# Modulation products moved from TensorE to VectorE, complex products by three real ones, and a new hand-written order in a one-layer S5, attention and MoE block

## The chip, the cores and the metric

The kernel runs on one core of a Trainium2 chip. The metric is the device time of one execution in microseconds; all numbers below are of that core. The engines are named as the profile names them: PE (TensorE matmul) with PEld (its weight load), DVE (VectorE), ACT (ScalarE), POOL (GpSimd) and SP (SyncE, which here only issues DMAs).

## The reference, cut to what matters

```python
def reference(x, c, ctx, c_ctx, w_mod, b_mod, w_in, s5_..., w_exp_gate, w_exp_up, w_exp_down, ...):
    sh1, sc1, g1, sh2, sc2, g2 = split(silu(c) @ w_mod + b_mod, 6)           # 6 x 1024 values
    sh1c, sc1c, ... = split(silu(c_ctx) @ w_mod + b_mod, 6)                  # only the first two are used
    h, hc = _modulate(x, sh1, sc1), _modulate(ctx, sh1c, sc1c)               # 256 x 1024 each
    u, q, k, v, gate_logits = split(h @ w_in); uc, _, kc, vc, _ = split(hc @ w_in)
    y_ssm = u * s5_d
    for d, reverse in enumerate((False, True)):                              # complex, 32 groups x 64 states
        ab, bb = _s5_discretise(a, log_dt, b)                                # powers of ab, products with b and c
        hc_ = _s5_scan(uc, ab, bb, reverse)                                  # context first ...
        hl_ = _s5_scan(u, ab, bb, reverse, init=hc_[edge])                   # ... its last state starts the latent scan
        y_ssm += real(c * hl_)
    o = attention(rope(rms(q)), [rope(rms(k)), rms(kc)], [v, vc])            # 8 heads, 2 kv heads, 512 keys
    mix = (sig(gate_s) * glu(gelu(y_ssm)) + sig(gate_a) * (o @ w_attn_o)) @ w_out
    x = _layer_norm(alpha * x + g1 * mix) * ln1_g + ln1_b
    x = _layer_norm(alpha * x + g2 * moe(_modulate(x, sh2, sc2))) * ln2_g + ln2_b   # 32 experts, top 2
    return x
```

So `sh2, sc2, g1, g2` (four of the six thousands of columns of `w_mod`) are wanted for `c` alone. Every weight is float32.

## The kernel before, in words

The 256 latent tokens are kept in two tiles of 128. There are two parts.

**The front** is the token sub-layer. It is written as 44 Python generators, each a chain of steps on some engines (`loads`, `mod1`, `mod2`, `u_flow` inside `dense`, `s5_powers`, `w1_flow`, `scan`, ...). `Flow.run` takes them by the list `Flow.ORDER`, 900 numbers long: each number says which generator takes its next step. Nothing is scheduled at run time: the list fixes the order of the instructions on every engine and of the DMAs on the queue of SP, and each engine works through its instructions in that order and waits at the head where data or a buffer is missing. Buffers are slots of a few tags: `p8` (5 of 8 KB a partition), `p4` (`N4` = 15 of 4 KB), `p2` (`N2` = 6 of 2 KB), `pe`, `t2`, and the weight slots `raw` (3 of 8 KB), `w`, `l4`, `g4` (4 each of 4 KB).

- `dense` is the main stream of matmuls: 264 steps, in this order: `u_flow` (steps 0 to 20), the k/v columns (to 52), q (to 84), the gate logits (to 156), the GLU (to 196), the attention output (to 232), the output projection (to 264). Its weights come by `loads` (SP) into `raw`, and `splits` makes a high and a low part of each (ACT copies, DVE subtracts), so that a product takes three matmuls.
- `mod_load`, `mod_loads`, `modmm`, `mod_cols`, `mod1`, `mod2`: the modulation. `w_mod` is loaded in blocks of 256 columns, and TensorE multiplies each by a 32-column tile `scp` that holds silu(c) and silu(c_ctx); ACT copies the result (`mr`), TensorE transposes it, and DVE reduces it into `modT`. `mod1` does the first 2048 columns (4 calls of `mod_cols`), `mod2` the other 4096 (8 calls, 16.8 MB, loaded into `g4`, in the trace `g<-in_w_mod_dram`).
- `s5_powers` makes powers of the diagonal (`pw`, `pin`, `pout`) and `bb`; `w2_flow` and `w1_flow` multiply them with the S5 matrices c and b, 8 blocks each, six DVE instructions of 512 elements a block (four products, two sums); `w1T_flow` transposes `w1` on TensorE, `state_in` multiplies with `U` (the S5 input, turned through HBM by `u_turn` on the queue of POOL), `scan` runs on DVE (a tree, then 31 steps in series), `states` copies, `k_flow` and `outputs` make the S5 output, which passes through HBM (`yscr`), gelu and into the GLU of `dense`.
- `scores`, `softmax`, `weigh`, `values` are the attention, worked in beside the rest; `residual`, `norm`, `stats`, `router`, `choose`, `gate1`, `diag2` the end of the front.
- `prefetch8`, `prefetch4`, `refill` load expert weights (`ew`) into slots that the front no longer needs.

**The MoE** is a plain loop over 16 pairs of experts (`for p in range(NP)`): gate and up products (`gu`), the down product (`y`), dispatch and combine. Each pair takes 12.6 MB of float32 weights; 201 MB in all go through a ring of all the slots (`first`), loaded by SP in the order of use as slots come free.

Of the kernel before, what the change touches and what calls it, by code (L numbers as in the profile page):

```python
# [8 lines left out]
FT = mybir.dt.float32  # L9
# [3 lines left out]
AF = mybir.ActivationFunctionType  # L13
# [19 lines left out]
N8, N4, N2, NPE = 5, 15, 6, 5  # L33
# [52 lines left out]
class Flow:  # L86
# [213 lines left out]
def build(ctx, tc, I, out):  # L300
# [88 lines left out]
    wm, loaded = [], []  # L389
# [15 lines left out]
    def loads():  # L405
# [1540 lines left out]
```

## Time and profile before

| | before |
|---|---|
| median of 3 runs | 819.25 us (819.23 to 820.12) |
| the profiled execution, device time | 820.36 us |
| its span, first to last instruction | 818.6 us (1.76 us lie around it) |
| mean granted clock of TensorE | 0.978 |
| PE / PEld / DVE / ACT / POOL busy | 94% / 53% / 45% / 36% / 4% |
| bytes moved by DMA | 269.73 MB, mean 330 GB/s |

A busy PE is not PE at its peak, since matmuls are pipelined and the recorded ends overlap. DVE's 45% is a mean of two unlike parts: it is near full in the first 100 us and little used in the MoE. The strip below the totals on the page (40 slices) shows that, and that DMA has gaps in the front and none after it.

### The profile page before, as it was taken

To read this page: it belongs to the slowest core of one execution; us is meant where nothing else is said; L and a number is where in the kernel's file an instruction comes from. 1 tells how busy PE (TensorE), PEld (TensorE's weight loads), DVE (VectorE), ACT (ScalarE), POOL (GpSimd) and SP (SyncE) were. 2 spreads that over 40 slices of the span, in tenths; PEclk is the share of its full clock that TensorE was granted. 3 is DMA by queue.
4 is the path that set the end of the run, shared out by engine and by line. 5 is a ranking of instruction groups with operands and counts; after the bars stand their busy time and mean duration, and the time that the engine had idled before them with its cause. 6 is when DMAs were issued, how large, how long until landed. Compare 5 with 4: busy or idle time off the path is not lost. (4 is left out here: it accounts for less than half of the span.)

```text
span 818.6 us, 11438 instructions
## 1 busy us (share of the span) xinstructions
PE 765.9 (94%) x4371; PEld 437.5 (53%) x4371; DVE 371.6 (45%) x857; ACT 295.3 (36%) x574; POOL 30.8 (4%) x48
## 2 busy tenths in 40 slices
PE   3999989989999999899999999999999999999994
PEld 1787777646667787644443444344344534444431
DVE  7999969877544767813211221122122122202115
ACT  5553586756988544522210221022022102202200
POOL 0004202000000000200000000000000000000000
PEclk9899999999999999899999999999999999999997
DMA  9977275593658686989999999999999999999992
GB/s 359 349 307 279 52 238 147 216 323 106 192 144 309 249 292 219 348 329 399 414 412 413 412 414 413 412 413 412 411 413 412 411 414 412 413 413 409 412 408 84
DMA packets 71138, 269.73 MB, mean 330 GB/s; under 512 B 12195, under 2 KB 17699, under 8 KB 59173
## 3 DMA queue, kind: packets, MB, share of 16 engines
q1 hardware_dynamic: 65268, 265.29, 83.7%
q0 software_dynamic: 1152, 2.59, 1.1%
q10 hardware_dynamic: 4656, 1.05, 0.6%
q8 instruction: 37, 0.61, 0.3%
q14 instruction: 25, 0.20, 0.1%
HBM read 265.79 MB, written 3.11 MB: 329 GB/s over the span
## 5 line engine op out<-in xcount | busy, mean ns | idle before, releaser
L238 PE MATMUL gu<-ew,x 128*64 128x512 f32 x1024 | 233.0, 602 | 4.4 <-PEq L1719 2.5
L238 PEld LDWEIGHTS gu<-ew,x 128*64 128x64 f32 x1024 | 75.3, 138 | 149.7 <-issue 134.5
L238 PE MATMUL y<-ew,hT 128*64 128x512 f32 x512 | 113.5, 595 | 0.8 <-DVE hT L238 0.8
L238 DVE TENSOR_TENSOR hh<-hh,gu 128x512 f32<-128x512 f32 x16 | 11.0, 688 | 212.1 <-PE gu L238 212.1
L238 ACT ACTIVATE x<-y,modT 128x128 f32<-128x128 f32 x120 | 45.1, 455 | 139.4 <-PE y L238 139.4
L238 DVE TENSOR_TENSOR wl<-raw,wh 128x1024 fp32r<-128x1024 f32 x52 | 63.4, 1223 | 28.7 <-ACT wh L238 28.5
L238 PEld LDWEIGHTS y<-ew,hT 128*64 128x64 f32 x512 | 36.3, 137 | 66.7 <-issue 63.6
L238 ACT ACTIVATE wh<-raw 128x1024 fp32r<-128x1024 f32 x52 | 54.9, 1059 | 25.2 <-PE acc L238 24.9
L238 PEld LDWEIGHTS y<-d,xh 128*128 128x128 f32 x480 | 55.9, 192 | 12.2 <-issue 10.5
L238 PE MATMUL acc<-wh,hh 128*128 128x512 f32 x128 | 57.3, 448 | 3.1 <-DVE q L238 2.0
L238 PE MATMUL y<-d,xh 128*128 128x128 f32 x480 | 60.0, 278 | 0.0
L238 ACT ACTIVATE yh<-x 128x512 fp32r<-128x512 f32 x32 | 20.1, 629 | 105.0 <-DVE x L238 105.0
L238 DVE SCALAR_TENSOR_TENSOR x<-y,wsl,g 128x512 f32<-128x512 f32 x32 | 24.0, 751 | 66.7 <-PE y L238 66.7
L238 ACT ACTIVATE hh<-gu 128x512 f32<-128x512 f32 x16 | 9.6, 597 | 123.4 <-PE gu L238 123.4
L238 PE MATMUL acc<-wh,hl 128*128 128x512 f32 x128 | 51.4, 401 | 0.0
L238 PE MATMUL acc<-wl,hh 128*128 128x512 f32 x128 | 51.3, 401 | 0.0
L238 DVE TENSOR_TENSOR yl<-x,yh 128x512 fp32r<-128x512 f32 x32 | 22.2, 692 | 24.1 <-ACT yh L238 24.1
L238 PEld LDWEIGHTS acc<-wh,hh 128*128 128x128 f32 x128 | 24.4, 190 | 11.8 <-issue 4.3
L238 PEld LDWEIGHTS acc<-wh,hl 128*128 128x128 f32 x128 | 24.5, 191 | 5.9
L238 PEld LDWEIGHTS acc<-wl,hh 128*128 128x128 f32 x128 | 24.5, 192 | 5.7 <-issue 1.2
L238 PE MATMUL acc<-yh,cw 128*128 128x512 f32 x64 | 27.0, 422 | 0.4 <-ACT yh L238 0.4
L238 PE MATMUL acc<-yl,cw 128*128 128x512 f32 x64 | 25.3, 395 | 0.2 <-DVE yl L238 0.2
(263 smaller groups left out, 1052.8 us busy)
## 6 DMA issues: line engine op xcount, KB each, us to landing
ew<-in_w_exp_gate_dram SPq DMA_DIRECT2D x92, 512.0 KB, 11.7
ew<-in_w_exp_up_dram SPq DMA_DIRECT2D x88, 512.0 KB, 11.4
ew<-in_w_exp_down_dram SPq DMA_DIRECT2D x84, 512.0 KB, 11.4
ew<-in_w_exp_down_dram SPq DMA_DIRECT2D x21, 1024.0 KB, 12.6
ew<-in_w_exp_up_dram SPq DMA_DIRECT2D x20, 1024.0 KB, 12.6
ew<-in_w_exp_gate_dram SPq DMA_DIRECT2D x18, 1024.0 KB, 12.5
g<-in_w_mod_dram SPq DMA_DIRECT2D x32, 512.0 KB, 6.7
raw<-in_w_in_dram SPq DMA_DIRECT2D x14, 1024.0 KB, 5.7
```

Of the source, the lines that this page charges most:

```text
L238: return f(*args, **kw)
```

## The change

- `mod2` no longer uses TensorE. `w_mod`'s last 4096 columns are stored transposed (`w_modT`), so that a tile of 128 partitions holds 128 columns, one a partition, with all 1024 weights of each along it. silu(c) is broadcast to all partitions (`cb`), and one DVE `tensor_tensor_reduce` of 128x1024 for each of 32 tiles multiplies and sums. The tiles are 512 KB each, in `p4`; the bytes are the same 16.8 MB.
- `w2_flow` and `w1_flow`: a complex product by three real products. A block now takes three DVE instructions (one of 512 elements, two of 1024). The operands for it (`pq`, `pin`, `pout`, `pone`, `sums`) are new: two additions on POOL, twelve copies of half the partitions on ACT in the place of four on DVE, two sums on DVE.
- The scratch for DMAs issued from POOL (`dynamic_dma_scratch_size`) goes from its default of 16 KB a partition to 2 KB; `N4` goes from 15 to 18, `N2` from 6 to 7.
- `prefetch4` runs over `(N4 - 4) // 2` pairs of tiles, so 7 pairs in the place of 5.
- The attention output product may start on its first half (`o_n[0] >= 2*(k//4)+2`).
- `ORDER` is another list, 895 numbers long.

```diff
-N8, N4, N2, NPE = 5, 15, 6, 5
+N8, N4, N2, NPE = 5, 18, 7, 5
...
-    ORDER = [1, 5, 1, 3, 4, 3, ...]
+    ORDER = [3, 1, 1, 3, 3, 4, ...]
...
     def mod_loads():
-        for o in ((3, 4), (2, 5)):
-            for jp in range(4):
-                yield ask("Z", None, lambda: m_l[0] == 4, lambda: U, g4=4)
-                wm.append([[wload(w_mod, z * D + 256 * jp, 256, k0, 4, "g4") for k0 in (0, 4)] for z in o])
+        for z in (1, 2, 0, 3):
+            for j in range(KT):
+                yield ask("Z", None, lambda: m_l[0] == 4, lambda: g_n[0] >= 15, p4=1)
+                r = new("p4", [P, D], name="wr")
+                SY.dma_start(r, I["w_modT"][z * KT + j])
+                wm2.append(r)
...
     def mod2():
-        for half in (1, 2):
-            for jp in range(4):
-                yield ask("T", None, lambda: mod_n[0] >= 4)
-                yield from mod_cols(half, jp)
+        yield ask("Y", None, lambda: m_l[0] == 4, lambda: g_n[0] >= 14, p4=1)
+        cb = new("p4", [P, D], name="cb")
+        bcast(cb, I["crow"], D)
+        yield ask("S", [cb], table=AF.Silu)
+        S.activation(cb, cb, AF.Silu)
+        for half, w in ((1, 0), (1, 1), (2, 0), (2, 1)):
+            sm = small.tile([P, KT], FT, name=f"msum{half}{w}", bufs=1)
+            for j in range(KT):
+                yield ask("V", lambda: [wm2[0], cb], lambda: wm2)
+                r = wm2.pop(0)
+                V.tensor_tensor_reduce(out=r, in0=r, in1=cb, scale=1.0, scalar=0.0, op0=OP.mult, op1=OP.add, accum_out=sm[:, j:j + 1])
+                free(r)
+            stt(modT[:, half, w, :, 0], sm, float(w if half < 2 else 0), bmodT[:, half, w], OP.add, OP.add)
+            md.add((half, w))
+        free(cb)
...
+        PL.tensor_tensor(out=pq[:, 0], in0=pw[:, 0], in1=pw[:, 1], op=OP.add)
+        PL.tensor_tensor(out=pq[:, 1], in0=pw[:, 1], in1=pw[:, 0], op=OP.subtract)
...
+        def put(o, src, w, sign=1.0):
+            for z, h in enumerate((H0, H1)):
+                S.activation(o[h], src[h, places[w, z]].rearrange("p m (b g) -> p b g m", g=4), AF.Copy, scale=sign)
...
     def w1_flow():
...
-            for r in range(2):
-                if r:
-                    yield ask("V")
-                tt(t1, pr[0], br[r], OP.mult)
-                yield ask("V")
-                tt(w1[r], pr[1], br[1 - r], OP.mult)
-                yield ask("V")
-                tt(w1[r], t1, w1[r], OP.add if r else OP.subtract)
-                w1q.append(w1[r])
+            sh = [P, 4, C, 8]
+            tt(t1, pone[0][:, 1, b, :, None, :].to_broadcast(sh), sums[0][:, 1, b, :, :, None].to_broadcast(sh), OP.mult)
+            yield ask("V")
+            sh = [P, 8, C, 8]
+            tt(w1.rearrange("p r g c j -> p (r g) c j"), pin[0][:, b].rearrange("p r g j -> p (r g) j")[:, :, None, :].to_broadcast(sh),
+               bb[0][:, b].rearrange("p r g c -> p (r g) c")[:, :, :, None].to_broadcast(sh), OP.mult)
+            yield ask("V")
+            wf = w1.rearrange("p r g c j -> p r (g c j)")
+            tt(wf, wf, t1.rearrange("p g c j -> p (g c j)")[:, None, :].to_broadcast([P, 2, 512]), OP.add)
+            w1q.append(w1)
...
-            ps = yield from gemm(8, lambda k: o_n[0] == 4 and [[x[:, k % 4, a] for x in oT[k // 4]] for a in A] or None, 2)
+            ps = yield from gemm(8, lambda k: o_n[0] >= 2 * (k // 4) + 2 and [[x[:, k % 4, a] for x in oT[k // 4]] for a in A] or None, 2)
...
-        yield ask("V", None, lambda: g1 and mod_n[0] == 12 and count)
+        yield ask("V", None, lambda: g1 and (2, 0) in md and count)
...
-    nc = _bacc.Bacc("TRN2", target_bir_lowering=False, num_devices=1)
+    nc = _bacc.Bacc("TRN2", target_bir_lowering=False, num_devices=1, dynamic_dma_scratch_size=2048)
```

What the two lists say of the order, counted in steps of `dense` that stand ahead (0 to 264):

| steps of | before | after |
|---|---|---|
| `mod_loads` (SP) | 5 to 95 | 88 to 229 (22 of 32 tiles by 154) |
| `mod2` | 7 to 130, on PE, ACT and DVE (3 of 8 blocks ahead of `scan`) | 97 to 247, on DVE (2 products ahead of the end of `scan`, 30 behind it) |
| `w2_flow` | 4 to 50 | 8 to 58 |
| `w1_flow` | 31 to 84 | 34 to 84 |
| `state_in` | 52 to 85 | 64 to 88 |
| `scan` | 85 to 130 | 76 to 127 |
| first reload of `kscr` by SP (`outputs`) | 52 | 104 |
| `prefetch4`, pairs of `ew` tiles | 164, 165, 165, 178, 204 | 156, 167, 175, 182, 221, 233, 252 |

## Rows read from the trace of the kernel before

**Rows 1.** The page's strip: 40 slices of 20.5 us; DMA's busy tenths, GB/s.
```profile
DMA  9977275593658686989999999999999999999992
GB/s 359 349 307 279 52 238 147 216 323 106 192 144 309 249 292 219 348 329 399 414 412 413 412 414 413 412 413 412 411 413 412 411 414 412 413 413 409 412 408 84
```

**Rows 2.** Busy time by stretch: us, busy (x instructions) of each engine, clock, DMA share, GB/s.
```profile
27.00:107.00 80.00, 75.29 (x693) 61.52 (x692) 75.55 (x161) 43.22 (x87) 14.15 (x24) 1.00 0.66 232
107.00:154.00 47.00, 41.41 (x263) 33.37 (x262) 37.26 (x75) 37.25 (x98) 8.11 (x8) 1.00 0.66 224
154.00:213.50 59.50, 56.02 (x330) 37.48 (x331) 49.32 (x195) 38.19 (x58) 0.00 (x0) 0.97 0.51 177
213.50:255.60 42.10, 40.37 (x317) 25.51 (x316) 16.55 (x29) 34.69 (x63) 0.00 (x0) 0.96 0.67 192
255.60:332.00 76.40, 75.35 (x334) 59.42 (x333) 54.56 (x74) 37.16 (x48) 1.52 (x1) 1.00 0.74 270
332.00:350.50 18.50, 14.76 (x76) 10.78 (x74) 14.71 (x63) 11.22 (x25) 3.45 (x5) 0.82 1.00 383
350.50:694.00 343.50, 340.95 (x1756) 154.04 (x1758) 73.07 (x139) 62.15 (x140) 0.00 (x0) 1.00 1.01 407
```

**Rows 3.** The chain that ended last, in the MoE: start, us, what.
```profile
662.05 2.04 PE acc L238 x8
689.42 2.04 PE acc L238 x8
...
694.86 10.18 DMA ew<-in_w_exp_down_dram
...
748.55 2.04 PE acc L238 x8
...
781.48 2.04 PE acc L238 x8
```

**Rows 4.** Tiles `sb` and `gTh`: ns min/median/max, first to last start in us.
```profile
L238 DVE TENSOR_TENSOR xs<-sb,ap x12: 184/345/419, 154.4 to 170.9; 128x256 f32<-128x256 f32 x6, 128x128 f32<-128x128 f32 x2, 128x64 f32<-128x64 f32 x2, 128x32 f32<-128x32 f32 x2
...
L238 PE MATMUL acc<-wh,gTh x32: 392/398/795, 255.6 to 282.2; 128*128 128x512 f32 x32
```

**Rows 5.** Timeline of DVE, 36.6 to 39.2 us: start, us, instruction.
```profile
36.63 0.68 DVE L238 TENSOR_TENSOR wt<-pout,s5c 128x512 f32<-128x512 f32 x1
37.23 0.69 DVE L238 TENSOR_TENSOR w<-pout,s5c 128x512 f32<-128x512 f32 x1
37.84 1.22 DVE L238 TENSOR_TENSOR wl<-l,wh 128x1024 fp32r<-128x1024 f32 x1
38.97 0.68 DVE L238 TENSOR_TENSOR w<-wt,w 128x512 f32<-128x512 f32 x1
```

**Rows 6.** Groups of DVE, ACT and POOL by shape: xcount | busy us, mean ns | idle before.
```profile
L238 DVE SCALAR_TENSOR_TENSOR x<-x,dnv,ln 128x1024 f32<-128x1024 f32 x2 | 2.5, 1274 | 0.0
...
L238 ACT ACTIVATE sb<-ss 64x256 f32<-64x256 f32 x32 | 19.9, 623 | 6.0 <-PE ss L238 5.6
...
L238 ACT ACTIVATION_READ_ACCUMULATOR q<-acc 128x1 f32 x16 | 3.5, 217 | 0.0
...
L238 POOL TENSOR_TENSOR kr<-kr,mhalf 128x2 f32<-128x2 f32 x4 | 4.1, 1020 | 23.9 <-DVE kr L238 23.9
```

**Rows 7.** Timeline of PE around one modulation block: start, us, instruction.
```profile
56.44 1.93 PE L238 MATMUL ss<-g,scp 128*32 128x256 f32 x32
58.31 0.39 PE L238 MATMUL acc<-hh,wh 128*128 128x256 f32 x1
```

**Rows 8.** SP's waits, in all: us, times, longest.
```profile
SPq L238 <- DVE wl L238: 99.5, 16, 12.7
...
SPq L238 <- DMA kscr<-kall: 31.0, 2, 30.6
```

**Rows 9.** Tile `U`: POOL's DMAs (ns, first to last start in us) and their landing.
```profile
L238 POOL DMA_DIRECT2D U<-uscr x4: 882/886/912, 79.0 to 81.7; - x4
...
DMA to landing us min/median/max: 4.1/4.6/4.7
```

More of the change, by code (lines that the diff above doesn't have):

```diff
@@ L388, in build @@
     s5b, s5c, tabs = [], [], []
-    wm, loaded = [], []
+    wm, wm2, loaded = [], [], []
     def mod_load(c0):
@@ L427, in loads @@
                 yield ask("Y", p4=1)
-                s5c.append(new("p4", [P, 2, G, C], name="s5c"))
+                s5c.append(new("p4", [P, 8, 2, 4, C], name="s5c"))
                 SY.dma_start(s5c[0], I["s5c"])
@@ L655, in build @@
     ps4 = [P, 4, 8, C]
-    pin, pout = [], []
+    pin, pout, pone, sums = [], [], [], []
     bb = []
@@ L759, in s5_powers @@
             yield ask("V")
-            tt(b_[:, r], dd[:, 0], dd[:, 1], OP.add if r else OP.subtract)
-            yield ask("V")
+            d0, d1 = (dd[:, z].rearrange("p (b g) c -> p b g c", g=4) for z in range(2))
+            if r:
+                stt(b_[:, :, 1], d0, -1.0, d1, OP.mult, OP.subtract)
+            else:
+                tt(b_[:, :, 0], d0, d1, OP.subtract)
+            yield ask("V", **({"p4": 1} if r else {}))
         free(dd, s5b[0])
+        sums.append(new("p4", [P, 2, 8, 4, C], name="sums"))
+        tt(sums[0][:, 1], b_[:, :, 0], b_[:, :, 1], OP.add)
         bb.append(b_)
@@ L772, in s5_powers @@
         ap_n[0] = 1
-    def tpow(pt_, g0):
-        return [pt_[:, r, :, g0:g0 + 4].rearrange("p j g -> p g j")[:, :, :, None].to_broadcast(ps4) for r in range(2)]
-    def tcol(b_, g0):
-        return [b_[:, r, g0:g0 + 4][:, :, None, :].to_broadcast(ps4) for r in range(2)]
     w2q, w2d = [], {}
     def w2_flow():
+        yield ask("V", lambda: [s5c[0]], lambda: s5c and sums)
+        tt(sums[0][:, 0], s5c[0][:, :, 0], s5c[0][:, :, 1], OP.add)
         for f, tag in ((1, "p4"), (0, "l4")):
             for b in range(4):
-                g0 = 16 * f + 4 * b
+                i = 4 * f + b
                 yield ask("V", lambda: [s5c[0]], lambda: s5c and bb, lambda: f or u_n[0], p2=1, **{tag: 1})
@@ L805, in w2_flow @@
         free(s5c[0], pout[0])
+        fl.free_after(2, pone[0], sums[0])
     k_n = set()
@@ L871, in w1_flow @@
         fl.free_after(2, bb[0])
+        fl.free_after(2, pone[0], sums[0])
     def w1T_flow():
@@ L1313, in owed4 @@
     def owed4():
-        return 3 * (not kT) + (not rt) + 2 - len(qT) + 2 * (not hs) + 3 * (not yT)
+        return 3 * (not kT) + (not rt) + 2 - len(qT) + 2 * (not hs) + 3 * (not yT) + 4 * (len(md) < 4)
     def owed8():
@@ L1396, in router_w @@
     def router_w():
-        yield ask("V", lambda: [modT, rt_[0]], lambda: rt_ and count and mod_n[0] >= 8, t2=1)
+        yield ask("V", lambda: [modT, rt_[0]], lambda: rt_ and count and (1, 1) in md, t2=1)
         sc, sh = (modT[:, 1, z, :, 0:1].to_broadcast([P, KT, 36]) for z in (1, 0))
@@ L1496, in diag2 @@
     def diag2():
-        yield ask("S", None, lambda: g2 and x_h[1], t2=2)
+        yield ask("S", None, lambda: g2 and x_h[1] and (2, 1) in md, t2=2)
         dgs.extend(new("t2", [P, 4, P], name="dg") for _ in range(2))
```

86 lines of the change are left out of this document (46 added, 40 removed).

## The prediction

> **What bounds the kernel now.** I read the page's strip first. Its DMA line has gaps in the first 17 slices and is full from slice 19 on, at 411 to 414 GB/s [rows 1]. So there are two parts with different limits, and I took the busy time by stretch to find where they part: up to 332 us TensorE is busy 75.3 of 80, 41.4 of 47, 56.0 of 59.5, 40.4 of 42.1 and 75.4 of 76.4 us, and DMA moves 177 to 270 GB/s; from 332 us DMA is full [rows 2]. Then the chain of waits says what ends the MoE. Its pairs of experts follow each other by 27.37 us (662.05 to 689.42), which is TensorE's own pace, until 694.86, where an expert weight's DMA is the releaser; after that two pairs take 59.13 us and one 32.93, 10.0 us more than three at 27.37 [rows 3]. The MoE is therefore nearly balanced: TensorE alone would end 10 us earlier, and what decides is when DMA becomes full for good and how many bytes had come by then. Both hang on the front: a front that ends d earlier takes the end with it by d, and expert weights that arrive ahead of 332 us are worth their bytes at 407 GB/s [rows 2], up to those 10 us.
>
> In the front two chains run beside each other. One is TensorE's bulk of products. The other is the S5: w1 blocks on VectorE, `state_in`, the scan from 154.4 us, then `outputs`, gelu, and the first GLU product at 255.6 us [rows 4], which `dense` reaches with TensorE 96% busy in the stretch ahead [rows 2]. From there to 350.5 us TensorE has hardly a gap. VectorE is as full as TensorE up to 107 us (75.55 of 80 us), loose behind 213.5 us (16.55 of 42.1, 54.56 of 76.4) [rows 2].
>
> **The change part by part.**
>
> *w1 and w2.* Six VectorE instructions of 512 elements follow each other by 0.60 us (36.63 to 37.23), one of 1024 takes 1.13 (37.84 to 38.97) [rows 5]. A block goes from 6 x 0.60 = 3.60 us to 0.60 + 2 x 1.13 = 2.86; 16 blocks save 11.8 us. The operand patterns (a broadcast along the last axis) are of the kind that the old products had, so I take no change of rate. The four old copies of 512 elements leave VectorE (2.4 us by the same 0.60), and two sums of that size come (1.2). Of `mod2`'s small reductions a few fall ahead of the scan, left at nothing. Net: VectorE loses 12 to 13 us ahead of the scan, in a stretch where it is 94% busy for 80 us and 79% for 47.
> The price is on other engines: twelve ACT copies of half the partitions, at most 0.62 us each as `sb` has it for 64x256 [rows 6], 7.5 us, in a stretch in which ACT is busy 43 of 80 us [rows 2]; two POOL additions of 288 elements, for which the trace has only tiny operations (1.02 us for 128x2 [rows 6]), so 1 to 6 us together; I take 2, because most of POOL's time there is empty (14.15 of 80 us). They are a delay in front of w2 only, while VectorE has `bb` to make; `w2_flow` begins at step 8 in the place of 4. At nothing, with 0 to 6 us as bounds.
>
> *mod2 off TensorE.* One block of 32 matmul records holds TensorE 1.87 us (56.44 to 58.31) [rows 7]; eight blocks are 15.0 us, with their transposes a little more. By the order before, three stand ahead of the scan (5.6 us), five between scan and GLU (9.4 us). All of it is off the main stream.
>
> *32 products on VectorE.* An instruction of 1024 elements with two inputs is 1.13 us from start to start [rows 5]; ACT's reading of a sum takes another 0.22 [rows 6], for VectorE no row shows one. So 36 to 43 us in all, 32 times 1.13 to 1.35. Two fall ahead of the scan's end (2.3 to 2.7 us), thirty behind it: 34 to 41 us, against 25.6 + 21.8 = 47.4 us that VectorE is idle from 213.5 to 332 us [rows 2]. I take them as hidden there. If that cover is gone, each us beyond it is on the path, since VectorE also makes the low parts of the weights that TensorE waits for.
> [...]
>
> *Queues.* The 32 row tiles leave the early SP queue (steps 5 to 95) for steps 88 to 229, and each waits for a free p4 slot; behind it stand the weights of `dense`. From 255.6 to 332 us DMA moves 270 of 407 GB/s [rows 2], so 76.4 us leave 10.5 MB. Ten row tiles (5.2 MB) and four more expert tiles (2.1 MB) move into that stretch: 7.3 MB, which fits. In the early queue the wait of 30.6 us for `kscr` [rows 8] goes, since its first reload stands at step 104 and not 52; that gives the loads room, and I count no gain.
>
> *Smaller scratch.* What it does to POOL's DMAs no row shows. If it held one of the four reads of `U` at a time, three would each wait 4.6 us for the one ahead [rows 9], so `U` would be there 13.8 us later. It was issued by 82 us and `state_in` begins at step 64 now, 12 steps later than before. 0 to 6 us; I take 0. Silu and broadcast of `cb`: one ACT instruction and a table, off the path.
>
> *Buffers.* The four expert tiles are loaded ahead of the MoE: 2.1 MB / 407 GB/s = 5.1 us. Bounds: 5.1 where DMA has the gaps that it has now, 0 where it is full already.
>
> **The sum**, against the profiled execution (820.36 us, 1.11 over the median). Scan start: VectorE gives 12.5 us and TensorE 5.6; neither is alone on the path between 107 and 154 us, so I take -9 (bounds -5 to -13, and +6 for operands or scratch). Scan to GLU: TensorE gives 9.4 us, but the series on VectorE has to give too, and it gains nothing but gaps, against two products in it; I take -4 (bounds +3 to -10). GLU to MoE: 0 (bounds +5 for VectorE's products among the weights' low parts, -2 for the freer order). Buffers: -5 (0 to -5). Sum -18, so 802.4 for that execution and 801.3 for a median. The new order as a whole is in the bounds: a list cannot be priced entry by entry from a trace.
>
> **The rivals.** (A) *TensorE's bulk decides and the S5 chain follows*: all 15.0 us go, transposes and gaps between blocks another 6, buffers 5: -26, 793. For it: TensorE is the busiest engine in all stretches. Against it: the serial part of the scan.
> [...]
> (C) *Slower: SP's queue.* Its place is step 156 to 264. Ten of the last raw weight loads now stand among row tiles and expert tiles; if p4 slots come late, or DMA is full, each raw comes later by what is ahead of it, on average 7.3 MB / 10 = 0.73 MB plus a slot's wait. At 407 GB/s 0.73 MB are 1.8 us; with one more us of waiting, 2.8 each and 28 in all, less nothing: 829. It decides as soon as the stalls exceed 18 us. For it: SP already waits 99.5 us for raw slots, up to 12.7 at once [rows 8]. Against it: the 10.5 MB of room, and weights that are split ahead of their use.
> (D) *The chain does not move* (the VectorE time saved ahead of the scan is given back as latency of the new operands and of other waits): only the buffers and some 2 us are left: 812 to 817.
>
> **How the numbers follow.** My forecast (-11 to -22, 797 to 809) has 0.48; A (788 to 797) 0.18; B 0.10, half of it below 817.6; C (821 to 832) 0.12; D 0.12, nearly all of it faster. A measurement of this kernel can tell some 0.2% from no change: 817.6 to 820.9 is "same". Faster: 0.48 + 0.18 + 0.05 + 0.11 = 0.82; same 0.03; slower 0.15. The range runs from 788 to 817: it holds A, the forecast, D and half of B, 0.83, and leaves C out.
>
> **What would show each step.** The scan's first instruction at 143 to 147 us instead of 154.4, and the first GLU product at 240 to 245 instead of 255.6; the first `gu` product of the experts near 337. [...] VectorE 85 to 95% busy between scan and MoE. DMA full from about 325 us, and a wait of TensorE for expert weights that is some 5 us shorter than 10. The forecast is wrong if the GLU starts at its old time (D), if TensorE has gaps in the last 100 us of the front that a raw weight or a low part ends (C, B), or if DMA is full well ahead of the MoE without the end moving.

## The result, and the profile after

The kernel after takes 826.14 us (median; 825.21 to 827.1), the kernel before beside it 820.12: 1.0067 [1.0048, 1.0086], slower by 0.7%. Forecast were 801.3 and a range of 788 to 817. The profiled execution of after has 827.1 us and a span of 825.3, 6.7 us more than the 818.6 of before.

Three marks of the forecast are in both traces: the first scan instruction, the first GLU product and the first `gu` product. With the end they cut the span into four parts, and the last column adds up to all that the forecast missed (827.1 - 802.4 = 24.7).

| part | before | after | change | forecast | missed by |
|---|---|---|---|---|---|
| start to scan | 154.4 | 149.3 | -5.1 | -9 | 3.9 |
| scan to GLU | 101.2 | 105.4 | +4.2 | -4 | 8.2 |
| GLU to `gu` | 94.9 | 98.2 | +3.3 | 0 | 3.3 |
| `gu` to the end | 468.1 | 472.4 | +4.3 | -5 | 9.3 |

Each column is one execution, and where the scan starts in it hangs on TensorE's clock. The kernel of the first experiment, `tail_slot`, is the program of after up to the last pair of experts, yet in its trace the scan starts at 145.3 us, the GLU at 252.0 and `gu` at 351.0, with a span of 817.4. Its four parts are 145.3, 106.7, 99.0 and 466.4: beside before -9.1, +5.5, +4.1 and -1.7. Busy time from 107 to 145 us, of after and then of `tail_slot` (columns as in [rows 2]):
```profile
107.00:145.00 38.00, 34.73 (x195) 29.20 (x194) 31.16 (x50) 30.19 (x84) 9.55 (x11) 0.87 0.34 107
```
```profile
107.00:145.00 38.00, 34.71 (x222) 28.36 (x221) 34.49 (x57) 34.15 (x91) 13.11 (x17) 1.00 0.41 136
```
In after TensorE's granted clock is 0.50 from 116.0 to 119.4 and from 126.2 to 133.0 us (the trace of after has no other values than 0.50 and 1.00); in `tail_slot` it is 1.00 there. The same busy time holds 195 products instead of 222, and the scan comes 4.0 us later. So the 3.9 us missed in the first row of the table are the clock's.

The strip of the page of after, 40 slices of 20.6 us; DMA's busy tenths and GB/s, to be laid beside [rows 1]:
```profile
DMA  9932423554888999969999999999999999999971
GB/s 356 376 158 102 158 76 133 171 178 170 249 329 306 372 375 404 369 248 395 413 411 413 413 414 413 409 412 413 409 412 413 413 409 413 413 411 414 409 288 56
```
Where before moves 307 and 279 GB/s in the third and fourth slice, after moves 158 and 102, and it stays at or under 178 up to the tenth; the row tiles that left that place fill the slices from the eleventh. From the twelfth DMA is at 306 to 404, long before the MoE, and at the eighteenth it falls to 248; between 345 and 375 us SP waits up to 12.6 us at once for PE to free a slot.

Busy time by stretch of after (columns as in [rows 2]), cut at its own marks: 149.3 is the scan, 204.5 the first product with a reloaded `tm`, 254.7 the GLU, 332.6 the end of the output projection:
```profile
27.00:107.00 80.00, 76.02 (x587) 61.83 (x586) 70.18 (x139) 49.94 (x97) 13.11 (x19) 0.98 0.48 176
107.00:149.30 42.30, 39.02 (x221) 32.79 (x221) 34.40 (x58) 33.92 (x91) 12.58 (x16) 0.88 0.37 120
149.30:204.50 55.20, 46.34 (x183) 30.16 (x184) 52.88 (x192) 45.50 (x63) 0.00 (x0) 0.97 0.50 160
204.50:254.70 50.20, 38.02 (x303) 23.77 (x302) 28.97 (x52) 31.37 (x57) 0.00 (x0) 0.91 0.90 307
254.70:332.60 77.90, 77.66 (x334) 60.72 (x334) 70.64 (x104) 39.73 (x51) 1.54 (x1) 0.97 0.94 363
```
PE, 94 to 96% busy behind the scan's start before [rows 2], is idle for 8.9 of 55.2 us and for 12.2 of 50.2. Its `mod2` work is gone, but the time behind the scan is not: the gap it left is not filled. DMA is at 307 GB/s in the stretch that held 192 before.

**The scan ends earlier by more than was forecast.** Tile `gs`, the series, of before and then of after (ns min/median/max, first to last start):
```profile
L238 DVE TENSOR_TENSOR gs<-ys,ys x31: 224/225/227, 172.1 to 213.4; 128x64 f32<-128x64 f32 x31
```
```profile
L238 DVE TENSOR_TENSOR gs<-ys,ys x31: 224/225/227, 165.4 to 198.8; 128x64 f32<-128x64 f32 x31
```
It ends 14.6 us earlier, where -9 and -4 had been forecast for the GLU. So the gain was there at 199 us, and by 254.7 only 0.9 us of it was left (in `tail_slot` 18.6 us at the end of the series and 3.6 at the GLU).

**First loss: the reloads of `tm`.** SP's own instructions in after (start, us from the first to the last issue, tile), with the row tiles `wr` around them; and what PE says of the reloads:
```profile
202.80 2.56 SPq L238 DMA_DIRECT2D wr<-in_w_modT_dram  x2
205.46 13.18 SPq L238 DMA_DIRECT2D tm<-kscr  x8
...
229.76 16.49 SPq L238 DMA_DIRECT2D wr<-in_w_modT_dram  x6
```
```profile
220.93 0.43 PE L238 MATMUL ss<-tm,U 128*32 128x128 f32 x8 [2.85 <-DMA tm<-kscr]
```
Eight issues take 13.18 us, with 6.8 us between the sixth (210.63) and the seventh (217.45). In the trace's records every DMA names the semaphore that tells of its landing, and the DMAs of SP and ACT have eight of them in turn (numbers 100, 101, 102, 104 to 107 and 109). ACT's first write of `yscr`, issued at 213.94 and landed at 217.43, has 107; the seventh reload has 107 too, and SP waits for 107 ahead of it. The second write, landed at 245.86, shares 101 with the row tile that SP issues at 245.92. So a reload needs nothing from `yscr`, and yet SP waits for it, here between 205 and 219 us and, at the second write, between 226 and 250 (us, times, longest; before has no such row in either place):
```profile
SPq L238 <- DMA yscr<-ysb: 6.3, 1, 6.3
```
```profile
SPq L238 <- DMA yscr<-ysb: 9.8, 1, 9.8
```
The products with `tm` begin 11.4 us earlier than before (204.5 for 215.9) and end 6.0 earlier (233.3 for 239.3).

**Second loss: the round trip of `y` through HBM.** Tile `ysb`, first in before, then in after (issues of the two writes of `yscr`, and their landing), and then, by the timeline of after, ACT and PE, which waited for it:
```profile
L238 ACTq DMA_DIRECT2D yscr<-ysb x2: 366/378/389, 227.3 to 242.1; - x2
...
DMA to landing us min/median/max: 3.2/3.4/3.5
```
```profile
L238 ACTq DMA_DIRECT2D yscr<-ysb x2: 367/378/388, 213.9 to 235.4; - x2
...
DMA to landing us min/median/max: 3.5/7.0/10.4
```
```profile
246.48 1.06 ACT L238 ACTIVATE wh<-raw 128x1024 fp32r<-128x1024 f32 x1 [9.75 <-PE ss L238]
...
254.66 0.79 PE L238 MATMUL acc<-wh,gTh 128*128 128x512 f32 x1 [9.03 <-ACT gTh L238]
255.25 0.63 PE L238 MATMUL acc<-wl,gTh 128*128 128x512 f32 x1
```
The last write is issued 6.7 us earlier than before, and its 256 KB land 10.4 us later instead of at most 3.5, behind row tiles of 512 KB: DMA moves 294 GB/s in that time, and 80 while the last write of before is under way. ACT, whose queue issues the read back (`yT`), stands 9.75 us for it; the row names PE, but PE had long been done. PE then stands 9.03 us. Its granted clock is 0.51 from there to 259.4 us and 1.00 behind it, and until then most of its products take 0.63 us instead of 0.40.

**Third loss: the end.** PE in the last pair of experts, before and then after, and SP's wait in after between 765 and 800 us:
```profile
783.46 10.72 PE L238 MATMUL gu<-ew,x 128*64 128x512 f32 x48
```
```profile
782.09 8.07 PE L238 MATMUL gu<-ew,x 128*64 128x512 f32 x34
795.74 5.04 PE L238 MATMUL gu<-ew,x 128*64 128x512 f32 x14 [5.58 <-DMA ew<-in_w_exp_up_dram]
```
```profile
SPq L238 <- DMA ew<-in_w_exp_up_dram: 11.3, 2, 10.0
```
Before, 48 products run in one piece; after, 34, a gap, and 14. In the program, SP's list of slots had an unused `p8` slot for this last up tile before; after, the gains of the last norm sit in one of the three `raw` slots, the list turns one place earlier, and the load gets the slot of a tile of the same pair, loaded four tiles ahead. It can start only when PE has used that tile. Nothing of this is in the diff's text.

### The profile page after: what moved, and what is told of

Its sections match the earlier page's. It is cut to its first block, busy times and chain, and to the rows that moved or that the text cites. A ratio compares the mean times of both kernels' runs of the same rounds, so it can differ in the third digit from the quotient of the medians.

```text
span 825.3 us, 10829 instructions
## 1 busy us (share of the span) xinstructions
PE 756.5 (92%) x4083; PEld 431.0 (52%) x4083; DVE 392.4 (48%) x851; ACT 307.5 (37%) x584; POOL 34.4 (4%) x50
## 5 line engine op out<-in xcount | busy, mean ns | idle before, releaser
L238 DVE TENSOR_TENSOR wl<-raw,wh 128x1024 fp32r<-128x1024 f32 x52 | 63.5, 1221 | 21.3 <-ACT wh L238 20.8
L238 PEld LDWEIGHTS y<-d,xh 128*128 128x128 f32 x480 | 55.9, 192 | 12.2 <-issue 11.4
L238 PE MATMUL acc<-wh,hh 128*128 128x512 f32 x128 | 59.4, 464 | 2.3 <-ACT gate L238 2.1
L238 DVE CUSTOM_DVE_ANT_0 wr<-wr,cb 128x1024 f32<-128x1024 f32 x32 | 38.7, 1217 | 4.3 <-DMA wr<-in_w_modT_dram 4.3
## 6 DMA issues: line engine op xcount, KB each, us to landing
ew<-in_w_exp_gate_dram SPq DMA_DIRECT2D x96, 512.0 KB, 10.2
ew<-in_w_exp_down_dram SPq DMA_DIRECT2D x18, 1024.0 KB, 11.4
ew<-in_w_exp_gate_dram SPq DMA_DIRECT2D x16, 1024.0 KB, 11.4
```

Source lines behind the costliest of these rows:

```text
L238: return f(*args, **kw)
```

## The experiments

Ratios are to the kernel before; spans are of the profiled execution.

### The last slot

```diff
+            if p == NP - 1 and tag == "raw":
+                tag = "p8"
```


> The changed kernel with one line more: in the last pair the load that would take a raw slot takes the p8 slot that is free by then. Theory 1 (a slot): the tile with the final gains has one of the three raw slots, so the last up weights of the last pair wait for the slot of up weights of the same pair; the wait of 10.0 us on the queue of SP goes, the last pair's gate and up products take 10.7 us as before the change and not 18.6, and the time falls by 8 us to 817.5-818.5. Rival (the transfers are late as a whole): the wait moves to the next load, and the time stays over 822.

Measured: 820.26 us, 1.0001 [0.998, 1.0021], span 817.4. The gap:
```profile
789.22 3.65 PE L238 MATMUL gu<-ew,x 128*64 128x512 f32 x14 [1.16 <-DMA ew<-in_w_exp_up_dram]
```
5.58 became 1.16, and the span is 7.9 us shorter. Of these 7.9 us the clock ahead of the scan has 4.0; from `gu` to the end it is 6.0 us (472.4 against 466.4), and by the ratios 0.66%, or 5.4 us. One slot of one load is worth the whole difference between the two kernels.

### The read back of y on SP's queue, alone and with the slot

```diff
-        S.dma_start(y_, yscr.rearrange("(i p) t -> p i t", p=P))
+        SY.dma_start(y_, yscr.rearrange("(i p) t -> p i t", p=P))
```


> The changed kernel with the load of yT issued by SP in the place of ACT, at the same place of the order. SP then waits for yscr, and four rows of w_mod stand behind it; ACT splits weights meanwhile. Theory 2 (round trip through HBM): yscr lands in 4 to 6 us and not 10.4, the first GLU product starts at 247 to 250 and not 254.7, TensorE's stall of 9.0 us ahead of it falls to 1 to 4, and the time falls by 4 to 7 us, to 819-822. Rival (VectorE's 32 products bound the stretch behind): the GLU starts earlier, but the experts' first product stays within 1.5 us of 352.9 as VectorE is 91 to 95% busy from 260 to 333 us; time 824-826.

Measured: 821.56 us, 0.9993 [0.9971, 1.0014], span 820.8; GLU at 247.5 instead of 254.7 (3.1 us of it by a scan that starts at 146.2, with a granted clock of 1.00 from 107 to 145 us), yet `gu` only at 347.6 instead of 352.9. SP stands in the place of ACT, so the row tiles behind it wait, the write lands in at most 6.2 us, and PE waits 2.5 instead of 9.0 us.

> The changed kernel with both edits. Theories 1 and 2 together: the two lie in different stretches and add, so 811-814, under the kernel before by 6 to 9 us. If theory 2's rival holds, 816.5-818; if theory 1's rival holds, 819-822.

Measured with both edits: 815.6 us, 0.9936 [0.991, 0.9962], span 813.6, a little above the 811 to 814 that were expected. By the ratios the two gains, 0.66% and 0.74%, give 1.31 together: they add.

### Are the products or their loads the cost?

Both kernels start from the one with both edits. First the products alone are cut to 8 of 1024 elements, then their loads too, so that most of `mod2` is left out.
```diff
-  V.tensor_tensor_reduce(out=r, in0=r, in1=cb, ...)
+  V.tensor_tensor_reduce(out=r[:, :8], in0=r[:, :8], in1=cb[:, :8], ...)
```


> The kernel of the run both with each of the 32 products on VectorE over 8 elements in the place of 1024 (so the modulation is wrong; all loads and waits stay). It prices VectorE's 38.7 us. Prediction of step 1 (hidden): within 1.5 us of 815.6. Theory 4 (two of them stand in the scan's series, and 25 in stretches where VectorE is 91 to 97% busy and makes the low parts of the weights): 2 x 1.2 us at the scan's end and up to some 5 behind it, so 3 to 7 us less, 808.5-812.5.

```diff
-                SY.dma_start(r, I["w_modT"][z * KT + j])
+                SY.dma_start(r[:, :8], I["w_modT"][z * KT + j][:, :8])
```


> As short_products, and each of the 32 row tiles is loaded in its first 8 columns only (4 KB in the place of 512 KB), so 16.8 MB of transfers are gone too. It prices what these transfers cost beside the products. Theory (the rows stand in SP's queue ahead of raw weights, kscr and yscr between 200 and 250 us): 3 to 6 us under short_products, and expert weights that come ahead of the MoE fill its buffers by 320 us. Rival (the DMA has room for them everywhere now): within 1.5 us of short_products.

Measured: 0.9899 [0.9872, 0.9925] for the products, 0.9758 [0.9734, 0.9781] with the loads. So the arithmetic costs 0.37% of 820 us, 3 us (the intervals of the two kernels overlap, so that it is not clear of zero), and the transfers 1.41%, 11.6 us, more than twice the expected 3 to 6. The GLU of the second, which answers to [rows 4]:
```profile
L238 PE MATMUL acc<-wh,gTh x32: 393/396/497, 238.6 to 262.9; 128*128 128x512 f32 x32
```
With the transfers gone the writes of `yscr` land in 3.2 us, the scan begins at 147.9, the GLU at 238.6 and `gu` at 335.3, and the span is 801.5. Of the 12.1 us that the span is under that of the kernel with both edits, 9.3 lie between scan and GLU (90.7 against 100.0). The forecast's time is that of this kernel: one with both edits, whose rows and products cost almost nothing.

### The order of writes, and rows held back

Three kernels on top of both edits. The first lets the first write of `yscr` wait until the eight reloads of `tm` are issued (`write` does the write that was there; one call stands behind the reloads of the second half, one at the end of it):
```diff
-            S.dma_start(bass.AP(tensor=yscr.tensor, ...), ysb)
-            free(ysb)
+            late.append((f, ysb))
+            if f:
+                write()
...
+            if f:
+                write()
```


> The kernel of the run both, and the first write of yscr (by ACT) stands behind the eight reloads of kscr (by SP) in the order and not ahead of them. Theory 3 (the DMAs of all queues share eight semaphores in turn, so a DMA waits for the one eight places ahead, and the seventh reload waited for that write): the eight reloads follow each other with no gap of 6 us, TensorE's wait of 4.3 us for tm goes, the last write of yscr is issued 2 to 4 us earlier, and the time is 2 to 4 us under that of both (815.6): 811.5-813.5. Rival (the work between, softmax and weight splits, sets the pace of the S5 outputs anyway): the wait turns up at the next step, and the time is within 1 us of 815.6.

Measured: 813.62 us, 0.9891 [0.9862, 0.992] (the profiled execution, 818.3, was its slowest). The eight reloads take 9.83 us instead of 13.11 in the kernel with both edits, SP has no wait for `yscr` among them, PE no longer waits for them, and the last write goes out at 231.0 instead of 238.6. Then it lands 12.9 us later, behind the row tiles. One wait took the place of the other, and the intervals of the two kernels overlap.

The second also moves four row entries of the list (places 603 to 622) behind the read back, and one product with them:
```diff
-  [..., 2, 2, 1, 25, ..., 2, 24, ..., 24, 24, 7, 22, 2, 25, 22, 7, ...]
+  [..., 1, 25, ..., 24, ..., 24, 7, 22, 25, 22, 7, 2, 2, 2, 2, ...]
```


> The kernel of the run yscr_late with four row tiles of w_mod (and one product) moved behind the load of yT in the order; no work is left out. Theory 5 (row tiles in flight delay kscr and yscr; that is most of the 11.5 us that short_rows took off): the last write of yscr lands in 4 to 6 us and not 12.9, the first GLU product starts at 239 to 243 us and not 250.3, and the time is 4 to 7 us under yscr_late: ratio to before 0.981 to 0.985. Rival (from 255 to 333 us DMA and VectorE are full, so what moves there comes back as late low parts): the GLU starts earlier, and the ratio stays at 0.987 to 0.990.

Measured: 818.2 us, 0.9968 [0.9945, 0.999], a miss for the theory and for its rival. The write lands in 5.1 us and the GLU begins at 244.6, but VectorE:
```profile
243.75 1.23 DVE L238 CUSTOM_DVE_ANT_0 wr<-wr,cb 128x1024 f32<-128x1024 f32 x1 [7.98 <-DMA wr<-in_w_modT_dram]
...
251.09 1.22 DVE L238 TENSOR_TENSOR gTl<-yT,gTh 128x1024 fp32r<-128x1024 f32 x1
```
VectorE stands 8 us for a row, and `gTl` and the low parts are queued behind it; PE waits 4.0 us for the one and 2.5 for the other. A row that is late holds more than its own product.

The third moves four more row entries behind the read back and four products behind `gTl` (same kind of edit).

> The kernel of the run rows_held with four more row tiles and four products moved behind the split of yT on VectorE (gTl). In rows_held VectorE, which works in order, stood 8.0 us at a row tile with the low part of the next weight and gTl behind it, and TensorE waited 4.0 and 2.5 us for these. Theory 7 (what took the gain in rows_held is that place in VectorE's order): no wait for gTl over 1.5 us, the first 32 GLU products take 25 to 28 us and not 33, the experts' first product comes at 341 to 346 us and not 350.8, ratio 0.982 to 0.988. Rival (from 255 to 333 us VectorE has not the room for 4 products more, 4.9 us beside 70 of 78 us): first product at 347 or later, ratio 0.990 to 0.997.

Measured: 811.56 us, 0.9882 [0.9849, 0.9916], and again, with more executions, 811.63 us and 0.988 [0.9851, 0.9909]. `gTl` now comes ahead of the products, PE waits 0.5 us for it, and `gu` begins at 345.5, as the theory had it:
```profile
245.27 1.23 DVE L238 TENSOR_TENSOR gTl<-yT,gTh 128x1024 fp32r<-128x1024 f32 x1 [4.07 <-ACT gTh L238]
...
247.55 1.22 DVE L238 CUSTOM_DVE_ANT_0 wr<-wr,cb 128x1024 f32<-128x1024 f32 x1
```
This is 0.9% faster than the kernel with rows held back alone, and the best kernel of this study: 1.2% faster than before, and by the two ratios (0.988 / 1.0067) 1.9% faster than after. From the kernels with the late write (0.9891) and with the copies on POOL (0.988, below) the measurement does not tell it apart.

### The parts alone, on the kernel before

> The kernel before with the scratch for POOL's DMAs at 2 KB in the place of 16 KB and nothing else. Prediction: 0 us within 0.2%. Rival: the four reads of U go one behind the other, U up to 13.8 us later, and the scan's first instruction after 154.4 us by up to 6.

`dynamic_dma_scratch_size=2048` alone: 820.66 us, 0.9998 [0.9979, 1.0016]. Nothing, as taken, though the trace of before had only the landing of `U` [rows 9] to say so.

```diff
-N8, N4, N2, NPE = 5, 15, 6, 5
+N8, N4, N2, NPE = 5, 18, 7, 5
-    ORDER = [...]
+    ORDER = [..., 37, ..., 37, ...]     # two more steps of prefetch4
```


> The kernel before with the small scratch, N4 = 18, N2 = 7 and the two more pairs of expert tiles (two entries more in the order), nothing else; the tile with the final gains falls on the slots of w here, so the last pair has no conflict. Prediction: -5 us (0 to -5), so 815.5 (815.5 to 820.7). Rival, by the second look at the rows (of the 10.0 us that the prediction read as a wait for weights only 4.4 are one, the rest is the matmuls for the final gains): -2 to -4.4 us, 816-818.5.

Scratch and buffers: 817.68 us, 0.9952 [0.9927, 0.9977], that is -3.9 us.

The next three stand on that kernel. The first has the S5 flows by three products, twelve ACT copies ahead of them (the S5 edits of the diff, with the old order's entries of the removed steps taken out and a few moved):
```diff
+        pq = new("p4", [P, 2, 9, G], name="pq")
...
+        put(pout[0][:, :, 0], pq[:, 0], 0, -1.0)
+        yield ask("S")
+        put(pout[0][:, :, 1], pq[:, 1], 0)
...
-    ORDER = [..., 16, 16, 5, 16, ...]
+    ORDER = [..., 16, 16, 16, 16, 16, 16, 16, 16, 5, 16, ...]
```


> The kernel of the run buffers_alone (ratio 0.9952) with the complex products by three real ones; modulation on TensorE and the order of before, apart from the steps that the new flows have more or fewer of. Prediction: VectorE gives 12 us ahead of the scan, and the scan's first instruction comes 5 to 9 us before 154.8; time 5 to 9 us less, ratio 0.984 to 0.989. Rival (the chain does not move, since TensorE's part ahead of the scan is as full): the scan starts within 2 us of 154.8, ratio 0.993 to 0.997.

Measured: 826.03 us, 1.0052 [1.0035, 1.0069]; the scan begins at 165.1, 10.3 us later than in the kernel it stands on (154.8). ACT, and VectorE behind it:
```profile
28.33 2.69 ACT L238 ACTIVATE pout<-pq 64x256 f32<-64x256 f32 x4
31.03 1.27 ACT L238 ACTIVATE pone<-pw 64x256 f32<-64x256 f32 x2
32.31 2.56 ACT L238 ACTIVATE pin<-pq 64x256 f32<-64x256 f32 x4
34.88 1.27 ACT L238 ACTIVATE pone<-pw 64x256 f32<-64x256 f32 x2
36.17 1.09 ACT L238 ACTIVATE hm<-xT,modT 128x256 f32<-128x256 f32 x2
...
37.95 0.69 DVE L238 TENSOR_TENSOR hl<-hm,hh 128x512 fp32r<-128x512 f32 x1 [9.88 <-ACT hh L238]
```
The twelve copies take 7.8 us in one row, `hm` and `hh` stand behind them, and VectorE stands 9.88 us for `hh`; this `hl` comes 7.9 us later than in the kernel that it stands on (30.05). The rest of the 10.3 us is not told apart; TensorE's granted clock, 1.00 there, is 0.75 here from 27 to 40 us, while it waits too. The copies have nearly the size that was taken (0.65 us each, 0.62 taken [rows 6]); in this order they are on the path.

The second has `mod2` by products, its rows in the old early places:
```diff
-                wm.append([[wload(w_mod, ..., "g4") for k0 in (0, 4)] for z in o])
+                for i in range(j, j + 4):
+                    r = new("g4", [P, D], name="wr")
+                    SY.dma_start(r, I["w_modT"][z * KT + i])
```


> The kernel of the run buffers_alone (ratio 0.9952) with mod2 by VectorE's products, the row tiles in the slots g4 and at the places of the order that the column blocks had; complex products as before. It parts the change of engine from the moving of the loads. Theory 6 (VectorE is 94% busy up to 107 us, and three blocks, 12 products of 1.2 us, stand there): the scan starts later by 5 to 12 us, against 15 us less on TensorE; time -3 to +6 against buffers_alone, ratio 0.992 to 1.003. Rival (the engine does not matter, only TensorE's bulk does): ratio 0.983 to 0.988.

Measured: 847.22 us, 1.0316 [1.0299, 1.0334], scan at 175.0, far beyond the 5 to 12 us that were expected. Sixteen products, 19.5 us, and not twelve stand ahead of the scan on VectorE, and the scan is 20.2 us later. The way to it (columns as above):
```profile
27.00:107.00 80.00, 65.71 (x530) 53.37 (x529) 73.58 (x147) 35.30 (x68) 10.06 (x16) 0.94 0.62 226
107.00:175.00 68.00, 53.74 (x295) 44.16 (x295) 57.83 (x115) 46.79 (x116) 12.21 (x16) 0.89 0.54 174
```
VectorE is the fullest engine, busy 131.4 of 148 us, PE 119.5. That fits VectorE as the bound; but the granted clock is 0.94 and 0.89 here and 1.00 in the kernel that it stands on, and what the clock adds is not told apart.

> The kernel of the run complex_alone with mod2 as in mod2_early. All of the change's parts are in it but the late row tiles and the new order. Theory 5 (it is the late row tiles that took the gain): the scan starts at 148 to 154, the GLU at 240 to 248, and the time is 10 to 16 us under before, ratio 0.980 to 0.988. Rival (VectorE's 38.7 us cost the same wherever they are): ratio over 0.990.

Both together: 851.93 us, 1.0371 [1.0353, 1.0388]. The expected gain did not come. The two costs nearly add up (1.0% and 3.6% over the kernel with the buffers, 4.2% together), and it is the new order, with its row tiles late and its products behind the scan, that brings 1.0371 back to 1.0067.

### The copies in the new order

On the kernel with the late write, the copies are cut to an eighth (the rest of the tables left at a constant):
```diff
-   S.activation(o[h], src[...]..., AF.Copy, scale=sign)
+   S.activation(o[h][:, :1], src[...]...[:, :1], AF.Copy, scale=sign)
```


> The kernel of the run yscr_late with each of the twelve ACT copies that make pin, pout and pone over an eighth of its columns (the rest is filled with a constant by POOL ahead of it, so the S5 is wrong). It prices the copies. Prediction of step 1: 0 (0 to 6 us), hidden. Theory 8 (ACT works in order, and with 7.8 us of copies in a row complex_alone had its modulation 8.4 us late and its scan 10.3 us late; in the new order they stand between other steps, and VectorE waits 3.6 us for one weight's high part): the scan starts 3 to 6 us before 148.3, and the time is 2 to 5 us under yscr_late (ratio 0.9891): 0.983 to 0.987.

Measured: 812.5 us, 0.9895 [0.9853, 0.9936], beside 0.9891: no difference that can be measured. The scan begins at 145.4 instead of 148.3, but the kernel with products behind shows 148.7 in one profiled execution (granted clock 0.87 from 107 to 145 us) and 145.6 in another (1.00), so those 3 us are no evidence.

On the best kernel, the copies on POOL:
```diff
-   S.activation(o[h], src[...]..., AF.Copy, scale=sign)
+   PL.tensor_scalar(o[h], src[...]..., sign, None, op0=OP.mult)
```


> The kernel of the run products_behind with the twelve copies for pin, pout and pone on POOL in the place of ACT, whole. Theory 8 (the copies hold up ACT, which works in order; POOL has nothing to do from 31 to 57 us): VectorE's wait for a high part at 42 us goes, the scan starts 2 to 4 us before 148.7, ratio 0.983 to 0.987 (products_behind 0.9882). Rival (a copy on POOL takes so long, 0.8 us or more for each of 12 one behind the other, that pin and pout come later than by ACT): the scan starts at 148.7 or later, ratio 0.988 or more.

Measured: 811.05 us, 0.988 [0.9852, 0.9907], the same as without. The scan begins at 144.4, against 145.6 of the execution without at the same clock (1.00 from 107 to 145 us). VectorE in after's order, first with the copies on ACT (the kernel after), then on POOL, with a row of POOL:
```profile
42.25 1.23 DVE L238 TENSOR_TENSOR wl<-l,wh 128x1024 fp32r<-128x1024 f32 x1 [3.63 <-ACT wh L238]
...
44.59 0.69 DVE L238 TENSOR_TENSOR sums<-bb 128x512 f32<-128x512 f32 x1
```
```profile
31.44 6.05 POOL L238 TENSOR_SCALAR pout<-pq 64x256 f32<-64x256 f32 x4
...
32.55 1.15 DVE L238 TENSOR_TENSOR hl<-hm,hh 128x512 fp32r<-128x512 f32 x1
...
44.34 1.11 DVE L238 TENSOR_TENSOR sums<-bb 128x512 f32<-128x512 f32 x1
```
The wait of 3.63 us for ACT is gone, but many VectorE instructions of 512 elements beside the copies take 1.1 us instead of 0.68.

## Why the prediction was wrong, point by point

- **Start to scan, -9 taken, -5.1 measured in the profile of after and -9.1 in that of `tail_slot`.** VectorE's instruction times were right, and at the full clock the sum is. What failed here is a term that the sum did not have: TensorE's granted clock, 0.50 for 10.2 us ahead of the scan in after, 4.0 us. That the sum comes out at the full clock is in part luck: -9 was chosen between 12.5 and 5.6, and "at nothing, 0 to 6" for the copies and sums, on the ground that ACT has room on average, holds only by the new order. An engine that works in order delays what is queued behind: alone, the edit cost 10.3 us, beyond the upper bound. The new order spreads the copies; VectorE still waits 3.63 us at 42.25, and what that costs is not settled, since neither shortening the copies nor moving them to POOL changed the time.
- **Scan to GLU, -4 taken, +4.2 measured (+5.5 in `tail_slot`).** This is the step that decided. The worry was the series, and it gained 9.5 us more than the scan's start did (14.6 less 5.1). The step that failed is a path that the sum did not have: `tm`, `yscr` and `yT`, three sets of short DMAs between scan and GLU that stand in line with the row tiles. Before, they cost little (the writes land in 3.5 us at most, the read back in 4.0).
- **Queues, 0 taken.** "7.3 MB, which fits" was counted against 255.6 to 332 us alone, and there it does fit: 363 x 77.9 us is 28.3 MB beside 270 x 76.4 = 20.6 before. The failed step is that only the ten row tiles behind step 154 of `dense` were looked at. The 22 ahead of it are issued by 246 us, and 17 of them, 8.9 MB, only from 199 on, ahead of and between the short DMAs. Taking the transfers away gives 11.6 us, most of it between scan and GLU.
- **GLU to `gu`, 0 taken, +3.3 measured.** The bound was +5, "for VectorE's products among the weights' low parts". Some 2 us of it are the slow products behind PE's pause (255.25 to 259.41 us for nine that follow each other by 0.23 at the full clock). With both edits, where PE pauses 0.95 us there, the part takes 96.6 us; with the products cut it takes 99.0, so the products are not the rest. Where that is from is not told apart.
- **Products hidden.** Right as far as can be told: 3 us, not clear of zero. Their size was right too:
```profile
L238 DVE CUSTOM_DVE_ANT_0 wr<-wr,cb 128x1024 f32<-128x1024 f32 x32 | 38.7, 1217 | 4.3 <-DMA wr<-in_w_modT_dram 4.3
```
 1217 ns each, as the subtraction of the same shape at 1221, and 0.08 us for reading a sum. The forecast gives B a chance of 0.10: no run shows the longer time that it stands on, and in its place the 32 products of after took 1202 to 1227 ns each.
- **Buffers, -5 taken, -3.9 measured** by the part alone. The mechanism was right. The 10.0 us of waiting read from the chain [rows 3] was too much: 4.4 of it stand in the two pairs of 59.13 us, and the third pair is long for other work, the rows of the last norm.
- **`gu` to the end, -5 taken, +4.3 measured.** Here a term was missing: 6.0 us for one slot at the very end (472.4 against 466.4). Without it the part is 1.7 us shorter than before, not 5. No row of before could give it; that the slots of the last pair depend on how many slots stand ahead, and that the change altered that number, could be read from the list of slots.
- **Rivals.** C had the sign and, by chance, nearly the time (829). Its mechanism is half right: SP's queue and the row tiles, yes; raw weights that come late, no. PE's wait for low parts between 200 and 333 us:
```profile
PEld acc L238 <- DVE wl L238: 0.6, 1, 0.6
```
 What came late were the S5's round trips. A is out: PE's `mod2` time did go (318.1 to 306.5 us busy up to 353 us), into idle time. D's condition, a GLU at its old time, holds (254.7), but by losses behind the scan; ahead of it only the clock took something back. Of what would show each step, one sign was right: DMA near full ahead of the MoE (and, at the full clock, a second, the scan between 143 and 147); and the sign named for a wrong forecast was there too, DMA full without the end moving.
- **What stays open.** Rows earlier, where DMA now carries 120 to 176 GB/s, with their products left late were not tried; each row would hold a 4 KB slot until its product. Why TensorE's clock fell in after and not in `tail_slot` is open too. And of the 11.6 us of the transfers, the edits to `yscr`, rows and products got back up to 4.6 (0.9936 to 0.988); where the rest goes is not told apart.

## What to carry to other kernels

Before counting bytes into the room of a stretch, list the short DMAs on which an engine waits in it, and see what will be queued ahead of each; a 256 KB trip costs by what stands before it (landed in at most 3.5 us before, in 10.4 in after). Price work that goes to a half-empty engine by what is queued behind it there, not by the engine's share. And when slots are added or a ring turns otherwise, follow the last loads of the ring to their slots: the end of this kernel had nothing to hide a wait, and one slot there cost 6.0 us. Read the granted clock beside every mark of a trace: 4 us of this one were the clock's and not the change's order of work.

## What the runs showed of the hardware

- A write of 256 KB lands in 3.2 to 3.5 us (before) with DMA at some 70 to 80 GB/s, and in 10.4 (after) and 12.9 us (late write) behind 512 KB loads, with DMA at 294 and 320 GB/s while it is under way.
- Issues on SP wait for DMAs of ACT's queue (6.3 and 9.8 us for `yscr` in after): in the trace's records the two queues have the same eight semaphores, 107 for the first write and the seventh reload, 101 for the second write and the row tile issued at 245.92.
- TensorE's granted clock can differ between two executions of the same instructions. In after it is 0.50 from 116.0 to 119.4 and from 126.2 to 133.0 us; PE had waited 0.86 us ahead of the first and 1.57 ahead of the second. In `tail_slot` the same two waits (0.85 and 1.58) are there and it stays at 1.00. Six of the twelve profiles with the new order have such a fall between 107 and 145 us (0.87 to 0.91 in the mean), and none of before, scratch alone and buffers alone.
- Behind 9.03 us of idling TensorE's granted clock was 0.51 from 254.7 to 259.4 us, seven products there took 0.63 us instead of 0.40, and it was 1.00 from then on.
- With the copies on POOL (1.4 to 1.66 us each for 64x256, `copies_on_pool`), VectorE instructions of 512 elements beside them took 1.11 and 1.15 us, and others of that size, some of them beside copies too, 0.68: what is lost is at most some 0.5 us an instruction, less than one such copy.
